# The prompt's own attention, one score step later: an edit of the order at the entry of an attention stage

## The chip, the cores and the metric

The kernel runs on one core of one Trainium2 chip. Time is device time in microseconds (us) of one execution, and the median of several runs is given. The core has five queues that work side by side, each strictly in its own order: TensorE (PE, with its weight loads shown as PEld), VectorE (DVE), ScalarE (ACT), GpSimd (POOL), and SyncE (SP), which issues the transfers. They wait for one another by semaphores.

## The reference, cut to what matters

The program is one layer of a mixer with an attention part. There are eight tiles of 128 latent tokens and one tile of 128 prompt tokens, four heads each. A latent token reads all 1,024 latent keys and 256 context keys in one softmax; a prompt token reads the 128 prompt keys only.

```python
def _block_attention(q_nope, q_ropes, key_sets):
    ...
        s = jnp.concatenate(logits, axis=-1).astype(jnp.float32) * ATTN_SCALE
        p = jax.nn.softmax(s, axis=-1).astype(v_all.dtype)
        return jnp.einsum('bhqk,bkhv->bqhv', p, v_all)
...
        attn = _block_attention(qn, (qr,), ((kn, kr, vv),))                                  # prompt
...
        attn = _block_attention(qn, (qr_rot, qr), ((kn, kr_rot, vv), (kn_c, kr_c, v_c)))     # latents
```

The values are kept in the low-rank form in which they come (128 numbers for each key); the product with the value weights `w_uv` is made afterwards, on the 128 sums of a head.

## The kernel before, in words

Before the attention lie the modulation, the projections and the group without attention (up to about 315 us of the span). Behind it lies the output projection. The attention is written as lists of steps, each with a cost; `merged` and `run` call the steps one after the other, and `later` puts the dependent instructions of other engines into the program at a time worked out from these costs. The whole part stands under a manual schedule of PE, ACT, DVE and POOL, and SP is in program order everywhere: every queue runs in the order in which the steps issued their instructions, and nothing is moved on the chip.

A latent head is a pair (tile, head). The first six are called H0 to H5 here: (0,0), (0,1), (0,2), (0,3), (1,0), (1,1). `score_steps` (L1509) gives three steps for each: two of 512 latent keys (five matmuls each, L1503 to L1507, into one of two buffers `s1`), and one of 256 context keys (the same five lines, into one half of `s2`). `softmax` (L1468) issues what follows:

- DVE takes the maximum of the 1,024 scores (L1478), then that of the 256 (L1481), and makes the shift `nb` from both (L1482).
- ACT makes two exponentials (L1488), the 256 first and then the 1,024, which frees the buffer `s1`.
- DVE adds the two sums (L1492) and takes the reciprocal (L1493).
- POOL multiplies all 1,280 probabilities by it (L1494).

A later stage takes two heads of a tile together (`value_steps`, L1534): four transposes on PE into one of two PSUM buffers (L1550), the rounded high part on ACT (L1554), the low part on DVE (L112, the helper `lo_of`), and the value products (L1574 to L1576). The prompt tile has four steps of its own in `own_steps` (L1673), kept in a list `own`:

- `own[0]`, the scores: 20 small matmuls. Then DVE takes the maxima (L1690), ACT makes four exponentials (L1694), DVE a reciprocal (L1699), POOL the multiplication (L1701).
- `own[1]`, the transposes of the probabilities (L1708, four on PE). ACT makes the high part `ph8` (L1711), DVE the low part `pl8` (L112).
- `own[2]`, the value products (L1722 to L1724, three on PE). ACT copies the result, `os8`, out of PSUM (L1728).
- `own[3]`, the product of `os8` with `w_uv` (L1737, eight on PE). DVE multiplies the result into `mixB` (L1739).

The scores of H0 and H1 and `own[0]` come first, with the last rotary transposes `q_rope_T(7)` (L1320; its last part on DVE is L1346). Then the loop runs over pairs of heads. Its first round (`c == 0`) has the scores of H2 and H3, with `own[1]` and `own[2]` put between them. Its second round has the scores of H4 and H5, `own[3]`, and the first transposes for H0 and H1:

```python
vs = value_stream(pairs[0])
merged(sc[:2] + own[3:] + vs[:1] + sc[2:3] + vs[1:2] + sc[3:5], [])
merged(vs[2:], sc[5:])
```

So PE does, from the third round's scores on: H2 (three steps), `own[1]`, H3 first and second, `own[2]`, H3 third, H4 first and second, `own[3]`, transposes 0, H4 third, transposes 1, H5 first and second, transposes 2, H5 third, value products 0, transposes 3, value products 1, transposes 4.

Of the kernel before, what the change touches and what calls it, by code (L numbers as in the profile page):

```python
# [94 lines left out]
def tile_hymba_step(ctx: ExitStack, tc: tile.TileContext, I, O):  # L95
# [12 lines left out]
    def closed(cm):  # L108
        cm.__exit__(None, None, None)

    def lo_of(lo, src, hi):
        V.tensor_tensor(lo, src, f32(hi), op=ALU.subtract)  # L112

    def pool_copy(out, in_):
        G.tensor_scalar(out, in_, 1.0, 0.0, op0=ALU.mult, op1=ALU.add)
# [96 lines left out]
    def merged(a, b):  # L212
        ta, tb = sum(x for x, _ in a) or 1.0, sum(x for x, _ in b) or 1.0
        ia = ib = 0
        da = db = 0.0
        while ia < len(a) or ib < len(b):
            if ib >= len(b) or (ia < len(a) and da / ta <= db / tb):
                da += a[ia][0]
                run(a[ia])
                ia += 1  # L220
            else:
                db += b[ib][0]
                run(b[ib])
                ib += 1
# [1095 lines left out]
    def q_rope_T(t):  # L1320
        need(("r", t))
        g, j = t // 3, t % 3
        srcs = rot[t]
        late = t >= 7
        tp = (pst if late else psa).tile([P, 512], F32, tag="t" if late else "acc", name=f"qrT{t}")
        for s_, src in enumerate(srcs):
            for pr in range(2):
                c0 = (2 * s_ + pr) * P
                T.transpose(tp[:, c0 : c0 + P], src[:, 2 * pr : 2 * pr + 2, :].rearrange("p h r -> p (h r)"), ident)
        n = len(srcs)  # L1330
        sl = slice(j * P, (j + 1) * P)
        d5 = qr[g].rearrange("p s (a b) t -> p s a b t", b=2)
        src = tp[:, : n * 256].rearrange("p (s a t) -> p s a t", s=n, a=2)

        def part(par):
            own = slice(64 * par, 64 * par + 64)
            oth = slice(64 - 64 * par, 128 - 64 * par)
            later(0.0, lambda: S.copy(d5[own, 2 - n :, :, par, sl], src[own]))
            if t == 7:
                later((2.2, 5.8)[par], lambda: low(own, oth))  # L1340
                return
            later(0.65, lambda: V.tensor_tensor(d5[oth, 2 - n :, :, par, sl], src[own], f32(d5[own, 2 - n :, :, par, sl]), op=ALU.subtract))

        def low(own, oth):
            par = own.start // 64
            V.tensor_tensor(d5[oth, 2 - n :, :, par, sl], src[own], f32(d5[own, 2 - n :, :, par, sl]), op=ALU.subtract)  # L1346

        later(0.1 if t == 7 else 0.6, lambda: part(0))
        later(0.15 if t == 7 else 1.2, lambda: part(1))
# [159 lines left out]
    def score_steps(t, h):  # L1509
        g, j = t // 3, t % 3  # L1510
        sl = slice(j * P, (j + 1) * P)
        a, b = qnh[g][:, h, sl], qnl[g][:, h, sl]
        unrot = qr[g][:, 1, h, sl]
        c_ = s2[:, h % 2, :]
        rot = qr[g][:, 0, h, sl]
        cell = {}

        def lat(half):
            if half == 0:
                cell["s"] = pss.tile([P, 2, 512], F32, tag="s1", name=f"s1{t}{h}", bufs=2)  # L1520
            logits(cell["s"][:, half, :], (a, b, rot), slice(half * 512, half * 512 + 512))
            if half == 1:
                cell["start"], cell["shift"] = softmax(t, h, cell["s"].rearrange("p a c -> p (a c)"), c_)
                later(1.2, cell["start"])

        def con():
            logits(c_, (a, b, unrot), slice(CTX0, CTX0 + 256))
            later(0.7, cell["shift"])

        return [(1.08, lambda: lat(0)), (1.08, lambda: lat(1)), (0.55, con)]  # L1530
# [77 lines left out]
    def split_job(hi, lo, key):  # L1608
        def low():
            lo()  # L1610
            made.add(key)

        def high():
            hi()
            later(1.6, lambda: los.append(low))

        his.append(high)
# [12 lines left out]
    def wo_piece(k, hi, lo):  # L1630
        woh[k], wol[k] = hi, lo
        loads.append((k, hi, lo))
        next_load()
# [26 lines left out]
    def wo_need(k):  # L1660
        while not made.issuperset((("w", k, 0), ("w", k, 1))):
            if los:
                spare_lo(1)
            elif waiting:
                now_, (due, fn) = now[0], waiting.pop(0)
                now[0] = due
                fn()
                now[0] = now_
            else:
                spare_hi(1)  # L1670
# [103 lines left out]
    with tc.manual_schedule(engines=engines):  # L1774
        mh, ml, xr, wps = {}, {}, {}, {}
        tail = []

        def mix_tiles(t):
            mh[t] = flat[0][4 + len(mh) % 2].rearrange("p (c q) -> p c q", c=8)
            ml[t] = wo.tile([P, 8, P], F32R, tag="ml", name=f"ml{t}", bufs=2)  # L1780
            sl = slice(t * P, (t + 1) * P)
            return [(mh[t][:, 4 * i : 4 * i + 4, :], ml[t][:, 4 * i : 4 * i + 4, :], src[:, :, sl]) for i, src in enumerate((mixA, mixB))]

        def mix_split(t):
            for hi, lo, src in mix_tiles(t):
                S.copy(hi, src)
                lo_of(lo, src, hi)

        def mix_jobs(t):
            for i, (hi, lo, src) in enumerate(mix_tiles(t)):  # L1790
                split_job(lambda hi=hi, src=src: pool_copy(hi, src), lambda hi=hi, lo=lo, src=src: lo_of(lo, src, hi), ("m", t, i))

        def out_terms(t, ps, c0, c1, ks):
            for k in ks:
                wo_need(k)
                a, b = mh[t][:, k, :], ml[t][:, k, :]
                T.matmul(ps, a, woh[k][:, c0:c1], start=k == 0, stop=False)  # L1797
                T.matmul(ps, a, wol[k][:, c0:c1], start=False, stop=False)  # L1798
                T.matmul(ps, b, woh[k][:, c0:c1], start=False, stop=k == NK - 1)  # L1799

        own = own_steps()
        first = [s_ for i in range(LEAD) for s_ in score_steps(*heads[i])]
        merged(first[:4] + own[:1] + [(0.45, lambda: q_rope_T(7))] + first[4:], [])
        for c in range(len(pairs)):
            sc = [s_ for i in (2 * c + LEAD, 2 * c + LEAD + 1) if i < len(heads) for s_ in score_steps(*heads[i])]
            if c == 0:
                sc = sc[:3] + own[1:2] + sc[3:5] + own[2:3] + sc[5:]
            if not sc:
                break
            if c == 1:  # L1810
# [3 lines that stand above are left out]
            else:  # L1814
                merged(sc, value_stream(pairs[c - 1]) if c > 0 else [])
            if 2 * c + LEAD + 1 == 11:
                closed(c_ra)
                c_wo, wo = opened("wo", side="left")
                for k in range(2):
                    wo_piece(k, *flat[0][2 * k : 2 * k + 2])  # L1820
                mix_jobs(8)
                mix_jobs(0)
            if 2 * c + LEAD + 1 == 23:
                for k in range(3):
                    wo_piece(2 + k, *flat[1][2 * k : 2 * k + 2])
        need(*[("e", *h) for h in heads[-2:]])
        closed(c_ps)
        c_pw, psw = opened("psw", bufs=5, space=PSUM)
        tail.append(1)
        for k, tags in ((5, ("kch", "kcl")), (6, ("krh", "krl"))):  # L1830
            wo_piece(k, *[kv.tile([P, 1024], F32R, tag=n, name=f"{n}{k}") for n in tags])
        wo_piece(7, *flat[2][0:2])
        for t in (8, 0):
            wps[t] = [psw.tile([P, 512], F32, tag="w", name=f"w{t}{i}") for i in range(2)]

        def load_xr(t):
            xr[t] = ep.tile([P, 1024], F32, tag="xr", name=f"xr{t}", bufs=4)
            nc.sync.dma_start(xr[t], I["x"][t])

        early = [  # L1840
            (0.65, lambda t=t, i=i, k=k: out_terms(t, wps[t][i], 512 * i, 512 * i + 512, [k]))
            for k in range(5) for t in (8, 0) for i in range(2)
        ]
        vs = value_stream(pairs[-2])
        merged(vs[:3], [])
        merged(vs[3:], early[:10])
        merged(value_stream(pairs[-1], drain=True), early[10:])
        catch_up(1e9)
# [181 lines left out]
```

## Time and profile before

| What | us |
|---|---|
| Median of three runs | 621.02 (620.98 to 623.31) |
| The profiled execution: span from the first to the last instruction | 620.5 |
| PE busy | 606.8 (98%) |
| PE weight loads busy | 549.0 (88%) |
| DVE busy | 411.3 (66%) |
| ACT busy | 298.9 (48%) |
| POOL busy | 123.2 (20%) |

The profile gives the span and no other time of its own for this execution; the median of the runs lies 0.5 us above the span. A line of the timeline has the start, the duration, the engine, the source line, the operation, the tile that is written and those that are read, the shape and the number of instructions merged; idle time ahead of it and what ended that stand in square brackets. Durations of matmuls overlap: the end of one is modelled, and the distance between two starts is the pace. A row of stretches gives the bounds, the length, the busy time of each engine (with the number of instructions), the granted clock of PE (1.00 is full speed), the share of the transfers and GB/s.

### The profile page before, as it was taken

What the parts mean: (1) busy time and instruction counts of PE and PEld (TensorE: products, weight loads), DVE (VectorE), ACT (ScalarE), POOL (GpSimd) and SP (SyncE); (2) the same over time, 40 slices, a digit from 0 to 9 for tenths busy, and PEclk for the clock granted to TensorE, in tenths of its full rate; (3) what the DMA queues carried; (4) which work ended last, traced back from release to release, by engine and by line L of the source; (5) the groups of instructions that cost most, each with busy time, mean ns of one, the idle gap of its engine ahead of it and who ended that gap; (6) DMA issues with size and microseconds to landing.
All of it is one profiled execution on the core that took longest, in us unless ns stands there. A gap on an engine that the chain in (4) does not pass through costs nothing.

```text
span 620.5 us, 9955 instructions
## 1 busy us (share of the span) xinstructions
PE 606.8 (98%) x3719; PEld 549.0 (88%) x3719; DVE 411.3 (66%) x938; ACT 298.9 (48%) x694; POOL 123.2 (20%) x167
## 2 busy tenths in 40 slices
PE   7999999999999999999999999999999999999995
PEld 6777889999989999999998899999999988888884
DVE  4685457997756468566778656767666754577655
ACT  6556764345433245455675565555555632232212
POOL 2461112000000000433364112323222241000001
PEclk8999999999999999999999999999999999999998
DMA  8992010100351133100010000000101113423311
GB/s 316 393 380 71 0 35 2 35 0 3 134 208 70 64 106 122 38 1 1 1 42 1 1 2 0 2 9 27 35 1 35 35 68 129 144 101 137 115 55 68
DMA packets 15327, 46.32 MB, mean 75 GB/s; under 512 B 1824, under 2 KB 4784, under 8 KB 14768
## 3 DMA queue, kind: packets, MB, share of 16 engines
q1 hardware_dynamic: 15136, 45.50, 20.7%
q8 instruction: 29, 0.48, 0.3%
q10 hardware_dynamic: 144, 0.20, 0.1%
q14 instruction: 18, 0.15, 0.1%
HBM read 40.87 MB, written 4.83 MB: 74 GB/s over the span
## 4 chain that ended last, share of the span: by engine, by line
PE 93%; DVE 3%; DMA 1%; ACT 1%; issue 1%; SPq 0%; ACTq 0%
PE p L953 10%; PE tp L751 8%; PE tp L975 5%; PE pT L1550 5%; PE w L1797 5%; PE w L1799 5%; PE w L1798 5%; PE s L1505 3%; PE s L1506 3%; PE s L1504 3%; PE s L1503 3%; PE o L1574 3%; PE s L1507 3%; PE o L1576 3%; PE o L1575 3%; PE zacc L1389 2%
## 5 line engine op out<-in xcount | busy, mean ns | idle before, releaser
L112 DVE TENSOR_TENSOR pl<-pT,ph 128x512 fp32r<-128x512 f32 x81 | 55.4, 687 | 48.8 <-ACT ph L1554 48.2
L1488 ACT ACTIVATE e<-s,nb,scl 128x256 f32<-128x256 f32 x64 | 56.1, 881 | 35.1 <-DVE nb L1482 35.1
L1494 POOL TENSOR_SCALAR e<-e,rs 128x1280 f32<-128x1280 f32 x32 | 43.0, 1343 | 130.2 <-DVE rs L1493 124.7
L1554 ACT CAST ph<-pT 128x512 fp32r<-128x512 f32 x80 | 45.5, 588 | 41.9 <-PE pT L1550 39.0
L751 PE MATMUL tp<-area,w 128*128 128x384 f32 x288 | 52.5, 338 | 0.0
L751 PEld LDWEIGHTS tp<-area,w 128*128 128x128 f32 x288 | 50.4, 188 | 0.4
L1550 PE MATMUL pT<-ident,e 128*128 128x128 f32 x320 | 48.0, 272 | 1.3 <-DVE pl L112 1.2
L1574 PE MATMUL o<-ph,vh 128*128 128x256 f32 x160 | 47.8, 299 | 0.0
L1576 PE MATMUL o<-ph,vl 128*128 128x256 f32 x160 | 44.9, 281 | 0.0
L1575 PE MATMUL o<-pl,vh 128*128 128x256 f32 x160 | 44.7, 280 | 0.0
L1799 PE MATMUL w<-area,ml 128*128 128x512 f32 (+1 forms) x114 | 43.2, 379 | 0.0
L1550 PEld LDWEIGHTS pT<-ident,e 128*128 128x128 f32 x320 | 37.4, 140 | 4.8 <-issue 1.6
L1478 DVE TENSOR_REDUCE m<-s 128x1 f32<-128x1024 f32 x32 | 38.9, 1217 | 1.5 <-PE s L1507 1.5
L1503 PE MATMUL s<-kch,area 128*128 128x512 f32 (+2 forms) x100 | 38.9, 389 | 0.0
L1236 POOL TENSOR_TENSOR kr<-z,rope 128x64 f32<-128x64 f32 x8 | 2.6, 321 | 172.0 <-ACT z L1245 172.0
L1506 PE MATMUL s<-krh,area 128*128 128x512 f32 (+2 forms) x100 | 35.4, 354 | 0.0
L1505 PE MATMUL s<-kch,area 128*128 128x512 f32 (+2 forms) x100 | 35.4, 354 | 0.0
L1504 PE MATMUL s<-kcl,area 128*128 128x512 f32 (+2 forms) x100 | 35.3, 353 | 0.0
L1507 PE MATMUL s<-krl,area 128*128 128x512 f32 (+2 forms) x100 | 35.1, 351 | 0.0
L975 PE MATMUL tp<-area,w 128*128 128x384 f32 x192 | 35.0, 337 | 0.0
L975 PEld LDWEIGHTS tp<-area,w 128*128 128x128 f32 x192 | 33.6, 188 | 0.4 <-issue 0.4
L1574 PEld LDWEIGHTS o<-ph,vh 128*128 128x128 f32 x160 | 30.1, 188 | 1.6
(375 smaller groups left out, 1601.1 us busy)
## 6 DMA issues: line engine op xcount, KB each, us to landing
ada<-in_ada_ss SPq DMA_DIRECT2D x16, 512.0 KB, 8.1
w2r<-in_w_t SPq DMA_DIRECT2D x12, 512.0 KB, 4.4
x<-in_x SPq DMA_DIRECT2D x9, 512.0 KB, 7.4
xr<-in_x SPq DMA_DIRECT2D x9, 512.0 KB, 4.0
adag<-in_ada_g SPq DMA_DIRECT2D x4, 1024.0 KB, 4.8
wor<-in_w_o SPq DMA_DIRECT2D x8, 512.0 KB, 3.4
out_y<-y SPq DMA_DIRECT2D x8, 512.0 KB, 4.8
wvr<-in_w_v SPq DMA_DIRECT2D x8, 256.0 KB, 9.2
```

The costliest lines, as they stand in the source:

```text
L112: V.tensor_tensor(lo, src, f32(hi), op=ALU.subtract)
L751: T.matmul(tps[i, g][:, :GW], w_[i][:, k, :], x_[k, g], start=k == 0 and j == 0, stop=k == NK - 1 and j == 2)
L953: T.matmul(banks[key], a_, b_, start=k == 0 and m == 0, stop=k == 3 and m == len(passes) - 1)
L975: T.matmul(tps[c, 2][:, :GW], w_[c][:, k, :], x_[k, 2], start=k == 0 and m == 0, stop=k == NK - 1 and m == 2)
L1488: S.activation(e[:, sl], src, AF.Exp, bias=nb, scale=scl[:, t : t + 1], accum_out=su[:, i : i + 1])
L1503: T.matmul(ps, qh_, kch[:, sl], start=True, stop=False)
L1505: T.matmul(ps, ql_, kch[:, sl], start=False, stop=False)
L1550: T.transpose(ps[:, w : w + P], es[t, h][:, c * P : (c + 1) * P], ident)
L1574: T.matmul(o, vh[:, kt, :], ph[:, sl], start=c == 0, stop=False)
L1575: T.matmul(o, vh[:, kt, :], pl[:, sl], start=False, stop=False)
L1576: T.matmul(o, vl[:, kt, :], ph[:, sl], start=False, stop=c == n - 1)
L1799: T.matmul(ps, b, woh[k][:, c0:c1], start=False, stop=k == NK - 1)
```

## The change

Only the order of the first round of the loop is changed. The transposes `own[1]` stand behind the first score step of H3, no longer ahead of it. The value products `own[2]` stand behind the third score step of H3, no longer ahead of it. What they issue on ACT and DVE moves with them. `own[3]` stays where it is.

```diff
             if c == 0:
-                sc = sc[:3] + own[1:2] + sc[3:5] + own[2:3] + sc[5:]
+                sc = sc[:4] + own[1:2] + sc[4:] + own[2:3]
             if not sc:
                 break
             if c == 1:
```

The instructions are the same in number and kind on every engine. Their order around the edit is this, for the queues that it changes:

| Queue | before | after |
|---|---|---|
| PE | H2 third, own[1], H3 first, H3 second, own[2], H3 third, H4 first | H2 third, H3 first, own[1], H3 second, H3 third, own[2], H4 first |
| ACT | exp H1, ph8, exp H2, os8, exp H3 | exp H1, exp H2, ph8, exp H3, os8 |
| DVE | rs H1, pl8, L1346, max H3 | rs H1, L1346, pl8, max H3 |
| DVE, later | max H4 (L1478), mixB (L1739), rs H3 | max H4 (L1478), rs H3, mixB (L1739) |

Here exp is L1488, max is L1478 and rs is L1492 with L1493. POOL and SP keep their order.

## The prediction

> **What bounds the kernel now.** I read the page first, for the bound; then stretches behind the entry; then the timeline of each engine between 324 and 343 us, row by row, because an edit of order is worth what the waits there are worth; last the granted clock.
>
> ```profile
> span 620.5 us, 9955 instructions
> PE 606.8 (98%) x3719; PEld 549.0 (88%) x3719; DVE 411.3 (66%) x938; ACT 298.9 (48%) x694; POOL 123.2 (20%) x167
> ```
>
> ```profile
> 360.00:380.00 20.00, 20.00 (x144) 18.61 (x143) 13.79 (x28) 10.76 (x22) 5.36 (x4) 1.00 0.00 1
> ```
>
> PE is the bound, and behind the entry it never stops (20.00 of 20.00 in this stretch). So what the entry gains or loses by about 346 us reaches the end of the program unchanged: nothing behind it has slack on PE to take it up, and no other engine is full there. The entry itself has two stops on PE:
>
> ```profile
> 327.10 0.66 PE L1708 MATMUL pT<-ident,e 128*128 128x128 f32 x4 [0.62 <-POOL e L1701]
> ...
> 331.21 0.40 PE L1503 MATMUL s<-kch,area 128*128 128x512 f32 x1
> ...
> 333.51 1.05 PE L1737 MATMUL at<-e,wuv 128*128 128x128 f32 x8
> ...
> 338.17 0.60 PE L1550 MATMUL pT<-ident,e 128*128 128x128 f32 x4
> ...
> 342.16 0.63 PE L1550 MATMUL pT<-ident,e 128*128 128x128 f32 x4 [0.95 <-DVE pl L112]
> ```
>
> The first stop (0.62) is the transposes of the prompt waiting for POOL. The second (0.95) ends with a low part on DVE. `own[3]` (L1737) starts at 333.51 without a wait. From it to the end of H5's second score step PE needs 338.17 - 333.51 = 4.66 us.
>
> **The change, part by part.** *The stop ahead of the transposes.* H3's first score step now comes first. It needs the buffer of H1, which the long exponential of H1 frees:
>
> ```profile
> 325.44 1.20 ACT L1488 ACTIVATE e<-s,nb,scl 128x1024 f32<-128x1024 f32 x1
> ...
> 327.80 0.59 ACT L1711 CAST ph<-pT 128x512 fp32r<-128x512 f32 x1 [1.07 <-PE pT L1708]
> ...
> 333.34 0.57 ACT L1488 ACTIVATE e<-s,nb,scl 128x256 f32<-128x256 f32 x1 [1.94 <-DVE nb L1482]
> ...
> 335.08 0.58 ACT L1554 CAST ph<-pT 128x512 fp32r<-128x512 f32 x1
> ```
>
> It ends at 325.44 + 1.20 = 326.64, so H3 starts at about 326.7 to 326.8, 0.3 to 0.4 us ahead of 327.10. The gain is 0.3 to 0.4 at most; the transposes then come at about 327.9, and their probabilities are ready (before, they were by 327.10). This gain is kept only if PE waits for nothing behind it.
>
> *ph8 and pl8.* On ACT `ph8` moves behind both exponentials of H2; on DVE `pl8` stays ahead of H3's maximum, so that maximum now waits for them.
>
> ```profile
> 327.52 0.22 DVE L1482 SCALAR_TENSOR_TENSOR nb<-m,nscl 128x1 f32<-128x1 f32 x1
> ...
> 328.47 0.69 DVE L112 TENSOR_TENSOR pl<-pT,ph 128x512 fp32r<-128x512 f32 x1 [0.46 <-ACT ph L1711]
> ...
> 330.11 1.23 DVE L1478 TENSOR_REDUCE m<-s 128x1 f32<-128x1024 f32 x1 [0.22 <-PE s L1507]
> 331.37 0.16 DVE L1492 TENSOR_TENSOR rs<-su 128x1 f32<-128x1 f32 x1
> ...
> 332.08 1.16 DVE L1482 SCALAR_TENSOR_TENSOR nb<-m,nscl 128x1 f32<-128x1 f32 x1
> ...
> 336.15 1.16 DVE L1482 SCALAR_TENSOR_TENSOR nb<-m,nscl 128x1 f32<-128x1 f32 x1
> 337.24 1.27 DVE L112 TENSOR_TENSOR pl<-pT,ph 128x512 fp32r<-128x512 f32 x2
> 338.43 1.21 DVE L1478 TENSOR_REDUCE m<-s 128x1 f32<-128x1024 f32 x1
> 339.56 0.14 DVE L1492 TENSOR_TENSOR rs<-su 128x1 f32<-128x1 f32 x1
> ```
>
> `nb` of H2 ends at 327.74, and nothing ahead of it changes. ACT is free, so H2's exponentials start at about 327.80 (0.10 behind `nb`, as at 333.34 behind 333.24, would be 327.84). The two take 335.08 - 333.34 = 1.74 until ACT begins the next: `ph8` 329.54 to 330.13. `pl8` 330.18 (328.47 stands 0.08 behind 327.80 + 0.59) plus 0.69: 330.87. H3's maximum starts about 0.1 ahead of that end, as at 338.43 ahead of 337.24 + 1.27: 330.78 in place of 330.11. The reciprocal's first part follows after 1.13 (339.56 - 338.43) to 1.26 (331.37 - 330.11): 331.95.
>
> *The value products on PE.* They need `pl8`: PE waits until about 330.92, does two of three matmuls (2 x 0.23; ten took 333.51 - 331.21), and starts H4 at 331.38 in place of 331.21. So the gain of 0.3 is gone already, and H4's scores end at 331.38 + (333.51 - 331.21) = 333.68.
>
> *os8.* This is the term that decides. On ACT `os8` now stands behind both exponentials of H3; these wait for `nb` of H3, and `nb` is held up by POOL:
>
> ```profile
> 331.89 1.34 POOL L1494 TENSOR_SCALAR e<-e,rs 128x1280 f32<-128x1280 f32 x1 [2.37 <-DVE rs L1493]
> ```
>
> `nb` took 0.22 at 327.52, but 1.16 at 332.08, and ended at 333.24, just as POOL's pass ended (331.89 + 1.34 = 333.23). POOL starts 331.89 - 331.37 = 0.52 behind the reciprocal's first part, and `nb` comes after that, now as before. So: POOL 332.47 to 333.81; `nb` ends 333.81; exponentials 333.91 (333.34 was 0.10 behind); `os8` 1.74 later, 335.65, and as long as the copy at 327.80, 0.59: 336.24. `own[3]` waits for it and starts at 336.29 in place of 333.51: 2.78 later. The small steps bound it: starts 0.03 to 0.12 behind an end and the 1.13 to 1.26 above give 336.21 to 336.48, a delay of 2.70 to 2.97. PE stands still from 333.68 to 336.29, 2.6 us.
>
> *mixB and the rest.* `mixB` moves behind H3's reciprocal on DVE and waits there for `own[3]`; behind it wait H4's second maximum, which needs PE's step after `own[3]` anyway, and the low parts of transposes 0. I cost it at nothing: POOL's pass for H3 then runs at about 336.4 to 337.7, ahead of H4's `nb`, which came 336.15 - 333.51 = 2.64 behind `own[3]` and so comes at 338.9; it then takes 0.22 and not 1.16. Without that cover `nb` stays as long as it was. L1346 moves ahead of `pl8` (nothing reads it soon). SP's and POOL's orders do not change, and no transfer is moved.
>
> *What is late next.* PE needs 4.66 to the end of H5's second step, plus 0.06 for starting after a wait (four transposes took 0.66 at 327.10, 0.60 at 338.17): 341.01. H5's maximum on DVE may start up to 0.1 sooner behind it than at 338.43, where two low parts ahead of it ended at 338.51; I take 0.06. From that maximum a chain on DVE (reciprocal, `nb` held by POOL, low part) leads to the second stop at 342.16, and every link hangs on that maximum. So the second stop stays, and does not take up the delay. Sum: 2.78 + 0.06 - 0.06 = 2.8 us, with bounds 2.7 to 3.0.
>
> **The clock.** A stop of 2.6 us raises a second question:
>
> ```profile
> 8.35:11.76 3.41, 1.60 (x19) 0.48 (x18) 1.67 (x7) 2.37 (x5) 1.33 (x1) 1.00 1.00 381
> 11.76:15.17 3.41, 3.01 (x14) 3.01 (x15) 2.59 (x4) 2.12 (x6) 1.52 (x2) 0.50 1.03 418
> 15.17:18.59 3.42, 3.42 (x13) 2.94 (x12) 3.00 (x10) 2.30 (x5) 0.00 (x0) 0.50 1.04 407
> ...
> 339.44:342.85 3.41, 2.46 (x22) 2.29 (x21) 2.51 (x6) 1.61 (x4) 1.33 (x1) 1.00 0.00 0
> ...
> 612.51:615.92 3.41, 0.56 (x5) 0.36 (x4) 2.37 (x8) 0.66 (x2) 0.96 (x1) 1.00 0.00 0
> ```
>
> PE's clock was granted at 0.50 in two stretches of this execution: from 11.76 to 18.59, and from 615.92 on. The first lasted 6.83, twice 3.41, and the two falls lie 604.16 apart, 177 times 3.413. So the clock is set at the ends of windows of 3.41 us that run through. A window with PE busy for 1.60 of 3.41 (47%) let it fall, one with 2.46 (72%) kept it, and after a fall it took one wholly busy window to come back. With a stop of 2.6 us a window is 24% busy if it holds all of it, and under 47% if it holds 1.8 of it. Where a window begins against the program I take as equally likely everywhere: at least 1.8 of the stop falls in one window in (0.8 + 2 x 0.8) of 3.41, 70%. At half speed for one window PE loses 1.7 us of work; 1.3 if the window begins up to 0.8 before the stop ends. Nearly all of it lies ahead of H5's second step (4.7 us of PE work), so it adds to the delay: 2.8 + 1.5 = 4.3 us.
>
> The Trainium skill ("TensorE: Matmul & The Clock Gate", Part 1, What's actually happening, and Why this matters for your kernels) has the clock fall after an idle window of about 3.4 us, and only gaps over about 3 us as harmful. The trace agrees on the length of the window (3.41), but its clock fell after one that was 47% busy; by the page's rule the stop here would be too short, and the time would be that of the first rival.
>
> **The rivals.**
>
> *The clock holds.* For it: only two windows of this trace tell what lets it fall, the 47% counts small matmuls at their modelled length, and the stop can lie across the end of a window, 1.3 on each side. Against it: the row of 47%. Time: 621.02 + 2.8 = 623.8, own range 623.6 to 624.1.
>
> *The clock stays low for two windows,* as at 11.76, where a window 88% busy did not bring it back. The window in which it fell here may hold the end of the stop. PE loses up to 1.7 more, less what the second stop (0.95) gives back: 626.4 to 627.
>
> *The delay is taken up (not slower).* If the second stop hung on DVE's own queue and not on H5's scores, it would give back 0.95 us and DVE's idle time. That decides only if `own[3]` is late by under about 1 us, that is if `os8` got through by 334.5. Against it: `os8` cannot start ahead of H3's exponentials, and those cannot start ahead of 333.24 even with the old times. Time: only the 0.3 of the first stop is left, 620.7.
>
> **How the numbers follow.** The sum stands against the profiled execution's span of 620.5; I add it to the median of the runs shown, 621.02, which is 0.5 above. Chances: fall for one window 0.50, clock holds 0.34, two windows 0.10, not slower 0.04, anything else 0.02. Forecast: 621.02 + 4.3 = 625.3, own range 624.9 to 625.8. The range 623.4 to 626.2 holds the first two cases and their bounds. About 0.5% (3.1 us, 624.1) is what a measurement of this kernel can tell from no change. The fall and its longer form lie above it (0.60), the upper end of the holding clock and half of the rest too (0.05): slower 0.65. The holding clock otherwise is within: 0.31. Faster: 0.04 (most of the last rival is even within).
>
> **What would show it.** Right: L1728 behind H3's exponentials and L1737 waiting for it about 2.5 us; L1711 behind H2's exponentials; L1723 waiting for L112 about 0.7; `nb` of H3 over 0.9 long; the second stop still there; all of PE 2.8 us later at transposes 4, or over 4 with a stretch at 0.50 near 336 to 341. Wrong: L1737 without a wait, the second stop gone, or a granted clock that never leaves 1.00.

## The result and the profile after

| | median us | runs |
|---|---|---|
| before | 621.83 (620.98 to 623.31) | 6 |
| after | 625.12 (623.87 to 626.44) | 6 |

The ratio after to before is 1.0057, with a 95% interval of 1.0042 to 1.0072: the changed kernel is slower by some 3.5 us.

The first lines of the page of the profiled execution after the change give the span and the busy time of each engine; the execution's own time is 625.27.

```profile
span 623.5 us, 9953 instructions
PE 607.4 (97%) x3719; PEld 549.1 (88%) x3719; DVE 410.0 (66%) x938; ACT 298.7 (48%) x694; POOL 123.0 (20%) x167
```

PE has the same 3,719 matmuls and 607.4 us of busy time (606.8 before), while the span is 3.0 longer. So PE has no more work; it stands still for longer. The view of PE's waits after the change (what it waited for, us in total, times, longest) says where:

```profile
PE at L1737 <- ACT e L1728: 2.3, 1, 2.3
...
PE pT L1550 <- DVE pl L112: 1.1, 2, 0.9
...
PE s L1503 <- ACT e L1488: 0.3, 1, 0.3
PE o L1723 <- DVE pl L112: 0.3, 1, 0.3
```

Before, the two rows of the attention were these:

```profile
PE pT L1550 <- DVE pl L112: 1.2, 2, 1.0
...
PE pT L1708 <- POOL e L1701: 0.6, 1, 0.6
```

The wait of 0.6 at the prompt's transposes is gone, a wait of 2.3 at `own[3]` (L1737) is new, and the second stop is where it was. The timelines of PE, ACT, DVE and POOL after the change answer to the rows that the prediction showed of before:

```profile
321.64 0.38 PE L1329 MATMUL qrT<-ident,qun 128*128 128x128 f32 x2
...
326.96 0.50 PE L1503 MATMUL s<-kch,area 128*128 128x512 f32 x1 [0.29 <-ACT e L1488]
...
330.41 0.41 PE L1722 MATMUL o<-ph,vh 128*128 128x512 f32 x1
331.11 0.50 PE L1723 MATMUL o<-pl,vh 128*128 128x512 f32 x1 [0.28 <-DVE pl L112]
...
331.68 0.39 PE L1503 MATMUL s<-kch,area 128*128 128x512 f32 x1
...
336.43 1.16 PE L1737 MATMUL at<-e,wuv 128*128 128x128 f32 x8 [2.31 <-ACT e L1728]
...
345.13 0.63 PE L1550 MATMUL pT<-ident,e 128*128 128x128 f32 x4 [0.91 <-DVE pl L112]
...
354.07 0.61 PE L1593 MATMUL at<-os,wuv 128*128 128x128 f32 x4
```

```profile
329.69 0.58 ACT L1711 CAST ph<-pT 128x512 fp32r<-128x512 f32 x1
334.06 0.56 ACT L1488 ACTIVATE e<-s,nb,scl 128x256 f32<-128x256 f32 x1 [3.78 <-DVE nb L1482]
...
335.79 0.58 ACT L1728 COPY e<-o 128x512 f32<-128x512 f32 x1
```

```profile
330.37 0.69 DVE L112 TENSOR_TENSOR pl<-pT,ph 128x512 fp32r<-128x512 f32 x1 [1.45 <-POOL e L1494]
330.97 1.21 DVE L1478 TENSOR_REDUCE m<-s 128x1 f32<-128x1024 f32 x1
332.10 0.15 DVE L1492 TENSOR_TENSOR rs<-su 128x1 f32<-128x1 f32 x1
...
332.81 1.15 DVE L1482 SCALAR_TENSOR_TENSOR nb<-m,nscl 128x1 f32<-128x1 f32 x1
...
339.11 0.22 DVE L1482 SCALAR_TENSOR_TENSOR nb<-m,nscl 128x1 f32<-128x1 f32 x1
```

```profile
332.62 1.34 POOL L1494 TENSOR_SCALAR e<-e,rs 128x1280 f32<-128x1280 f32 x1 [2.92 <-DVE rs L1493]
```

The reader follows the chain from the end. `own[3]` starts at 336.43, just behind `os8` (335.79 + 0.58 = 336.37). `os8` stands on ACT behind the two exponentials of H3, the first of which starts at 334.06. That waits for `nb` of H3, which took 1.15 and ended at 332.81 + 1.15 = 333.96, the moment at which POOL's pass ended (332.62 + 1.34). POOL waited for the reciprocal, that for H3's maximum on DVE, and that for `pl8`.

How much the entry lost can be read inside the traces, free of all that comes before it. The entry is measured from the last two rotary transposes (L1329, one row, 321.47 before, 321.64 after) to the first product of a latent pair with `w_uv` (L1593). That one was at 351.11 before:

```profile
321.47 0.38 PE L1329 MATMUL qrT<-ident,qun 128*128 128x128 f32 x2
...
351.11 0.61 PE L1593 MATMUL at<-os,wuv 128*128 128x128 f32 x4
```

The entry took 29.64 before and 32.43 after: 2.79 longer. The same measure is given for each experiment below, beside the ratio of its times. Up to `own[3]` it is 12.04 before (333.51 - 321.47) and 14.79 after, 2.75 longer.

### The profile page after: what moved, and what is told of

Same layout as the page of the kernel before. It is cut to its first block, busy times and chain, and to the rows that moved or that the text cites. A ratio compares the mean times of both kernels' runs of the same rounds, so it can differ in the third digit from the quotient of the medians.

```text
span 623.5 us, 9953 instructions
## 1 busy us (share of the span) xinstructions
PE 607.4 (97%) x3719; PEld 549.1 (88%) x3719; DVE 410.0 (66%) x938; ACT 298.7 (48%) x694; POOL 123.0 (20%) x167
## 4 chain that ended last, share of the span: by engine, by line
PE 92%; DVE 3%; DMA 1%; ACT 1%; issue 1%; SPq 0%; POOL 0%; ACTq 0%
PE p L953 10%; PE tp L751 8%; PE tp L975 5%; PE pT L1550 5%; PE w L1797 5%; PE w L1799 5%; PE w L1798 5%; PE o L1574 3%; PE s L1505 3%; PE s L1506 3%; PE o L1576 3%; PE s L1504 3%; PE s L1503 3%; PE s L1507 3%; PE o L1575 3%; PE zacc L1389 2%
## 5 line engine op out<-in xcount | busy, mean ns | idle before, releaser
L1488 ACT ACTIVATE e<-s,nb,scl 128x256 f32<-128x256 f32 x64 | 56.0, 880 | 37.4 <-DVE nb L1482 37.4
L1478 DVE TENSOR_REDUCE m<-s 128x1 f32<-128x1024 f32 x32 | 38.9, 1216 | 1.9 <-PE s L1507 1.9
```

Of the source, the lines that this page charges most:

```text
L1488: S.activation(e[:, sl], src, AF.Exp, bias=nb, scale=scl[:, t : t + 1], accum_out=su[:, i : i + 1])
```

## The experiments

### The changed kernel again, in more runs

No edit; the runs ask for the size of the change and for the granted clock.

> The changed kernel once more, beside the kernel before on the same chip, for the size of the change and for the clock. If only the queues count: 2.8 us over before in all runs alike (+0.45%), granted clock 1.00 around 326 to 350 us. If the clock also falls in some executions, depending on where its window of 3.41 us begins: runs in two groups, about +2.8 and +4.3, and a lower mean clock (by about 0.003) in the long ones.

Measured: 625.46 us (six runs) against 621.55 (24 runs of the kernel before), ratio 1.0063 (1.0047 to 1.0079). The entry took 32.45. The clock stayed at full speed through the stop. So the result repeats; the 2.8 us of the queues are there in both traces, and the fall of the clock in neither. Two groups some 1.5 apart cannot be made out in the six spans (623.0 to 625.0).

### The transposes alone

```diff
-                sc = sc[:4] + own[1:2] + sc[4:] + own[2:3]
+                sc = sc[:4] + own[1:2] + sc[4:5] + own[2:3] + sc[5:]
```

This stands against the changed kernel: `own[1]` is late, and `own[2]` is where it was before.

> Only the transposes own[1] stand one score step later; the value products own[2] stay between H3's second and third step. On ACT the copy os8 is then ahead of H3's exponentials, as before. If os8's place is the cause: own[3] (L1737) starts without a wait, and what is left is the wait of the value products for pl8 (behind H2's exponentials on ACT): PE at H4's first step 331.98 in place of 331.21, +0.7 us in all. If the cause is that pl8 holds up H3's maximum on DVE (and so H3's exponentials): nearly all of the 2.8 us stays.

Measured: 622.80 us (12 runs), ratio 1.0019 (1.0006 to 1.0031). The entry took 30.51, 0.87 more than before. The timelines of PE and ACT of this kernel:

```profile
329.64 0.49 PE L1722 MATMUL o<-ph,vh 128*128 128x512 f32 x1 [0.35 <-ACT ph L1711]
330.42 0.50 PE L1723 MATMUL o<-pl,vh 128*128 128x512 f32 x1 [0.29 <-DVE pl L112]
...
333.87 1.05 PE L1737 MATMUL at<-e,wuv 128*128 128x128 f32 x8
```

```profile
331.18 0.59 ACT L1728 COPY e<-o 128x512 f32<-128x512 f32 x1 [1.60 <-PE o L1724]
333.36 0.56 ACT L1488 ACTIVATE e<-s,nb,scl 128x256 f32<-128x256 f32 x1 [1.60 <-DVE nb L1482]
```

Now `os8` stands ahead of H3's exponentials, and `own[3]` doesn't wait. What is left is PE waiting for `ph8` and then for `pl8`, and the transposes' own stop has turned into a wait of 0.29 for H1's exponential.

### The value products alone

```diff
-                sc = sc[:4] + own[1:2] + sc[4:] + own[2:3]
+                sc = sc[:3] + own[1:2] + sc[3:] + own[2:3]
```

> Only the value products own[2] are moved, behind H3's third score step; the transposes stay where they were, so that ph8 and pl8 and H3's maximum are as before. os8 is behind H3's exponentials on ACT. If os8's place is the cause: own[3] waits from 333.5 to about 335.7, 2.2 us, and the kernel is 2.2 us longer. If pl8 ahead of H3's maximum is the cause: no change (within 0.3 us).

Measured: 624.89 us (7 runs), ratio 1.0056 (1.0036 to 1.0077); the entry took 31.88, 2.24 more. The timeline of PE of this kernel:

```profile
328.80 0.66 PE L1708 MATMUL pT<-ident,e 128*128 128x128 f32 x4 [0.62 <-POOL e L1701]
...
337.39 1.16 PE L1737 MATMUL at<-e,wuv 128*128 128x128 f32 x8 [2.07 <-ACT e L1728]
```

Both stops stand, the old one and the new one. So the products behind H3's third step are what puts `os8` behind H3's exponentials. The two halves don't add up: 0.87 + 2.24 = 3.11, both together 2.79. With the products late too, PE doesn't wait for `ph8`, and what it loses to `pl8` lies ahead of the longer wait for `os8`, which takes it up.

### The product with `w_uv` out of the way

```diff
-                merged(sc[:2] + own[3:] + vs[:1] + sc[2:3] + vs[1:2] + sc[3:5], [])
+                merged(sc[:2] + vs[:1] + sc[2:3] + vs[1:2] + sc[3:5] + own[3:], [])
```

This is the changed kernel with `own[3]` behind H5's second step. If the wait for `os8` is the cost, giving PE other work meanwhile must take it away.

> The changed kernel with own[3] moved too: behind H5's two large score steps, so that PE has other work while os8 waits on ACT. If PE's stop at own[3] is what costs: L1737 starts without a wait, and the kernel comes back to about +0.4 us over before; what is left is DVE's chain to transposes 4, with H4's shift (L1482) now under POOL's pass again. If the delay sits in the chain of H3's exponentials itself and not in PE's stop: it stays at +2 us or more.

Measured: 621.99 us (12 runs), ratio 1.0004 (0.9993 to 1.0015), no change from before; the entry took 30.07, 0.43 more. The timeline of PE of this kernel:

```profile
336.93 1.05 PE L1737 MATMUL at<-e,wuv 128*128 128x128 f32 x8
...
339.68 0.39 PE L1574 MATMUL o<-ph,vh 128*128 128x256 f32 x1 [0.67 <-DVE mixB L1739]
```

`own[3]` starts without a wait. The products behind it now wait 0.67 for `mixB`, which is late instead. That is more than the 0.43 that is left; on the other side the second stop, 0.95 before, is gone in this kernel.

### The POOL pass of H2 one step later

```diff
-            later(2.5 if t == 0 or (t, h) < (1, 2) else 1.9, divide)
+            later(4.2 if (t, h) == (0, 2) else 2.5 if t == 0 or (t, h) < (1, 2) else 1.9, divide)
```

The changed kernel again, but the reciprocal and division of H2 come into the program later, so that `nb` of H3 stands ahead of them. The link by which POOL held `nb` is cut, and the reciprocal's two small instructions no longer stand ahead of `nb` either.

> The changed kernel with the reciprocal of H2 (L1492, L1493) behind H3's shift (L1482) on DVE, so that POOL's pass over H2's probabilities starts after the shift. If POOL's pass holds up the shift: L1482 of H3 takes 0.22 us in place of 1.15, H3's exponentials, os8 and own[3] come about 1.3 us sooner, and the kernel is about 1.5 us over before in place of 2.8. If the shift is long for a reason of its own: it stays at 1.15, and only the 0.3 us of the two small instructions ahead of it are won.

Measured: 624.09 us (12 runs), ratio 1.0034 (1.0022 to 1.0046); the entry took 31.21, 1.57 more instead of 2.79. The timelines of DVE and PE of this kernel:

```profile
332.88 0.22 DVE L1482 SCALAR_TENSOR_TENSOR nb<-m,nscl 128x1 f32<-128x1 f32 x1
```

```profile
335.57 1.16 PE L1737 MATMUL at<-e,wuv 128*128 128x128 f32 x8 [1.08 <-ACT e L1728]
```

`nb` takes 0.22 in place of 1.15, and the wait at `own[3]` falls from 2.31 to 1.08. Counted from L1329, `nb` ends 1.20 sooner than in the changed kernel: 0.93 of it is POOL's hold (1.15 less 0.22), and 0.27 is its earlier start (10.90 in place of 11.17 behind L1329), with the reciprocal out of its way. So the hold on DVE is 0.9 of the 2.8.

### The order of before, with both of its stops removed

The same idea, applied to the kernel before:

```diff
-                later((2.2, 5.8)[par], lambda: low(own, oth))
+                later((5.2, 5.8)[par], lambda: low(own, oth))
...
-            later(2.5 if t == 0 or (t, h) < (1, 2) else 1.9, divide)
+            later(4.2 if (0, 2) <= (t, h) < (1, 1) else 2.5 if t == 0 or (t, h) < (1, 2) else 1.9, divide)
```

The first line moves a low part of the last rotary transposes on DVE (the one ahead of the prompt's softmax), the second the divisions of H2 to H4.

> The kernel before, with two edits of the order on DVE: the first of the two L1346 behind the reciprocal of the prompt's sums (L1699) and H2's shift, and the reciprocals of H2, H3 and H4 (L1492, L1493) behind the shift (L1482) of the head after them. If the two stops of PE in the kernel before come from this order, the stop at the transposes (0.62) shrinks to about 0.2, the shifts take 0.22 in place of 1.16, the stop at transposes 4 (0.95) goes, and the kernel is about 1.5 us faster than before (-0.25%). If the stops have other causes: no change.

Measured: 620.30 us (12 runs) against 621.56 (23 runs), ratio 0.9973 (0.9961 to 0.9985): faster than both kernels. The entry took 27.87, 1.77 less than before. In the view of PE's waits of this kernel, only this row of the attention is left, a wait at 504.15, far behind the entry:

```profile
PE pT L1550 <- DVE pl L112: 0.2, 1, 0.2
```

So the stop of 0.62 can be had back without moving the transposes, and the second stop of 0.95 came from the order on DVE as well. The shifts `nb` of H3 and H4 take 0.22 here, so the hold by POOL is gone with it; the two edits were not tried one by one, and what each is worth is not shown.

### Twelve stops of known length

The kernel before with stops put into PE's queue ahead of later pairs: a transpose, 8 to 18 copies of its result on ACT, and a transpose of the copy, for which PE waits. The results aren't used.

```diff
+        def stop(c, n):
+            ps = pst.tile([P, 512], F32, tag="t", name=f"stop{c}")
+            T.transpose(ps[:, 0:P], ident, ident)
+            d = ap_.tile([P, 512], F32R, tag="ph", name=f"dz{c}", bufs=4)
+            for _ in range(n):
+                S.copy(d[:, 0:P], ps[:, 0:P])
+            T.transpose(ps[:, P : 2 * P], f32(d[:, 0:P]), ident)
...
+            if c >= 3:
+                run((0.0, lambda: stop(c, (8, 11, 14, 18)[c % 4])))
```

> The kernel before with twelve stops on PE, one ahead of each round of the attention from the fourth to the fifteenth: PE transposes a block, ACT copies it 8, 11, 14 or 18 times, PE transposes the copy. PE stands still for about 1.5 to 4 us each time, at places that fall differently against the clock's window of 3.41 us. It computes the same and does more. If a window with PE busy for under about half lets the clock fall: stretches at 0.50 behind every stop that leaves a window under about 47% busy, some eight of the twelve, each costing up to 1.7 us beside the stop. If only a window that is idle, or nearly, does: none, or only behind stops over 3 us.

Measured (one run): 693.2 us. The stops were 2.50, 3.39, 4.28 and 5.47 us, three of each, longer than expected, and the clock fell after all twelve. So no window between 35% and 50% busy was tried in the attention. Rows of stretches of this kernel: the second begins where the granted clock falls and ends where it comes back, the first and third are the windows of 3.41 beside it, and the first holds the larger part of a stop of 2.50:

```profile
375.53:378.95 3.42, 1.21 (x6) 1.04 (x7) 0.29 (x2) 3.20 (x11) 0.00 (x0) 1.00 0.00 0
378.95:382.36 3.41, 3.41 (x17) 3.22 (x16) 0.92 (x3) 1.07 (x3) 0.33 (x1) 0.50 0.02 5
382.36:385.78 3.42, 3.42 (x26) 3.23 (x26) 2.24 (x3) 1.55 (x3) 1.01 (x1) 1.00 0.00 0
10.31:13.72 3.41, 2.18 (x24) 1.24 (x25) 1.52 (x4) 2.02 (x4) 2.36 (x2) 1.00 1.04 420
```

A window 35% busy (1.21 of 3.42) let the clock fall, for one window. So a stop of 2.5 us, about the length of ours (2.31), can do it. The last row is of the program's start, the window ahead of a fall at 13.72: there a window with PE 64% busy by the profile, with small matmuls of 128x32, fell as well.

### The stop filled with matmuls

```diff
+        def filler():
+            ps = pst.tile([P, 512], F32, tag="t", name="filler")
+            for i in range(10):
+                T.matmul(ps, vh[:, NS, :], kch[:, 0:512], start=i == 0, stop=i == 9)
...
-                merged(sc[:2] + own[3:] + vs[:1] + sc[2:3] + vs[1:2] + sc[3:5], [])
+                merged(sc[:2] + [(0.0, filler)] + own[3:] + vs[:1] + sc[2:3] + vs[1:2] + sc[3:5], [])
```

The changed kernel with ten matmuls, whose result isn't used, in the place of the stop: the same delay, but PE busy.

> The changed kernel with ten further matmuls (128x512, about 2.3 us, result unused) on PE between H4's second score step and own[3], where PE otherwise stands still for 2.3 to 2.7 us. The queues and own[3]'s start stay as in the changed kernel; only PE is busy in the stop. If the clock falls behind the stop in some executions and that is what lifts the measured change from 2.8 to 3.5 to 3.9 us: the kernel is 2.8 us over before (+0.45%), no longer, and some of its runs have a mean clock of 0.995 or more, as before's do. If the clock has no part in it: 3.5 to 3.9 us over before, as the changed kernel.

Measured: 625.15 us (9 runs), ratio 1.0039 (1.0024 to 1.0054). The entry took 32.42, as in the changed kernel. The timeline of PE of this kernel:

```profile
334.17 2.43 PE L1804 MATMUL filler<-kch,vh 128*128 128x512 f32 x10
336.65 1.16 PE L1737 MATMUL at<-e,wuv 128*128 128x128 f32 x8
```

In the mean of the spans this kernel lies 2.7 above the kernel before (622.76 against 620.06), the changed one 3.4 (623.45). The 0.7 between them has the sign that a falling clock would give, but it is no more than such a comparison of 9 and 14 runs can tell. The mean clocks point the same way, as the first of the two expectations has it: three of these nine executions have 0.997 and one 0.993, while of the 14 of the changed kernel one has 0.996 and eight 0.993 to 0.994.

### The clock in further executions, and the stop moved against the windows

These two are the changed kernel without an edit, for the clock at the stop.

> The changed kernel, one more execution with a profile, to see a stop that lies otherwise against the clock's window. The rule so far (windows with PE busy for 35% or less fell, 50% or more held): a stretch at 0.50 behind the stop at own[3] if a window has under about 45% there, none otherwise. From the entry to transposes 4, 2.8 us more than before without the stretch, about 4.3 with it.

> As the look before it: the changed kernel, one more execution with a profile. A stretch at 0.50 behind own[3]'s stop if a window has PE busy for under about 45%, and then about 4.3 us more than before from the entry to transposes 4; none and 2.8 us otherwise.

Measured: 625.52 and 624.08 us. In neither did the clock fall at the stop. The row of the window ahead of a possible fall, in the first and in the second:

```profile
332.65:336.07 3.42, 1.74 (x8) 1.10 (x6) 2.75 (x4) 1.76 (x5) 1.34 (x1) 1.00 0.00 0
```

```profile
331.15:334.56 3.41, 1.78 (x8) 1.13 (x6) 2.80 (x4) 1.71 (x4) 1.34 (x1) 1.00 0.00 0
```

With 51% and 52% busy the clock held. The end of a window cut the stop in two in both, as in the first profile of the changed kernel, where the two windows around it were 50% and 82% busy:

```profile
332.41:335.83 3.42, 1.70 (x8) 1.08 (x6) 2.74 (x4) 1.77 (x5) 1.34 (x1) 1.00 0.00 0
335.83:339.24 3.41, 2.81 (x23) 2.78 (x24) 1.56 (x5) 1.28 (x4) 1.33 (x1) 1.00 0.02 5
```

Nine matmuls were then put ahead of the attention's first scores, in the changed kernel and in the one before, to move the stop by 2 us against the windows:

```diff
+        def ahead():
+            ps = pst.tile([P, 512], F32, tag="t", name="ahead")
+            for i in range(9):
+                T.matmul(ps, kch[:, 0:P], kch[:, 0:512], start=i == 0, stop=i == 8)
+
+        run((0.0, ahead))
```

> The changed kernel with nine further matmuls (128x512, about 2.1 us, result unused) on PE ahead of the first scores of the attention. They move the stop at own[3] by 2.1 us against the clock's window, whose ends lay near 332.4, 335.8 and 339.2 in the profiles that showed no fall. The stop then lies at about 336.1 to 338.5, all in one window, which is some 30% busy. If the clock's window decides: a stretch at 0.50 of 3.4 us behind the stop in the profile if its window begins as in those, and from own[3] to transposes 4 about 1.6 us more than in the changed kernel (there 8.70). If stops of 2.3 us never let the clock fall: granted clock 1.00, and 8.70.

> The kernel before with the same nine matmuls at the same place, as the measure for the shifted changed kernel: about 2.1 us over before or less, where another engine hides a part. The shifted changed kernel should lie 2.8 us above it without a fall of the clock, and up to 4.5 where the clock falls.

Measured: 629.59 us (5 runs) in the changed order, ratio to the kernel before 1.0122 (1.0104 to 1.014), and 624.37 (6 runs) in the order of before, ratio 1.0051 (1.0032 to 1.007). The entry took 32.45 and 29.64, as without the nine. But the nine also waited 1.14 for a part of the keys, so the shift was about 3.5 us (L1329 comes 10.16 behind L1368 in place of 6.67), a whole window, and the stop was cut in two again (2.28 and 2.23 of 3.41 busy). The profile shows no fall. So this pair doesn't tell what a stop in one window does. Its two kernels lie 4.3 apart in the mean of 5 and 6 runs (5.2 by the medians), where their entries differ by 2.81; at the same mean clock, 0.990 to 0.991, the spans lie 3.0 apart (627.97 in three runs, 624.95 in two).

## Why the prediction was right, and where it was not

The side was right, and the time of 625.3 was met within 0.2; but of its two terms only the queues are shown, and that the time came so close is in part luck.

- *The first stop.* The gain of 0.3 to 0.4 came, and was spent at once. H3 started at 326.96; less 0.17, by which this execution reached the entry later, that is 326.79 (the forecast stands in brackets, here and below: 326.7 to 326.8). It waited there 0.29 for H1's exponential.
- *ph8 and pl8.* In the same reckoning `ph8` started at 329.52 (329.54), `pl8` at 330.20 (330.18), H3's maximum at 330.80 (330.78).
- *The products.* The low-part product started at 330.94 (330.92), H4 at 331.51 (331.38). The wait shows as 0.28, not 0.7: the matmul ahead of it is drawn 0.41 long, and only the 0.70 between the two starts, against a pace of 0.23, tells the loss of about 0.5.
- *os8, the term that decides.* POOL started at 332.45 (332.47), the exponentials at 333.89 (333.91), `os8` at 335.62 (335.65), `own[3]` at 336.26 (336.29). It is late by 2.75 where 2.78 was said. The wait of PE there is drawn 2.31 long and not 2.6: H4's scores began 0.13 later than said, and the last matmul ahead is drawn 0.39 long where the pace is 0.23. The value products alone, the late `own[3]` and the late division each change the entry as this chain says, so the chain is shown and not only argued.
- *What is late next.* The second stop stayed (0.91), `nb` of H4 fell to 0.22, `mixB` cost nothing (H4's second maximum behind it still waited 0.34 for PE), and the entry ended 2.79 late: the sum of 2.8 was right. The rival in which the delay is taken up fell.
- *The clock: the step that the traces don't bear out.* The prediction added 1.5 for one window at half speed, as the likeliest course. None of the four traces of the changed kernel, nor that of its shifted form, shows a fall; the term measured 0 there. The row it was built on, 47% busy at the program's start, counts small matmuls, and a window there 64% busy fell as well, while at the entry 50% to 52% was enough to hold. So the bound of 1.8 us of stop in one window, and the chance of 70% worked out from it, had no fair row. An estimate from the rows of the runs: with a stop of 2.31, a fall where 2.21 of it lies in one window (the row that fell) and none where 1.72 does (the row that held), the same sum gives 38 to 67%. It still takes every place of the window as equally likely, and in all five of these traces a window's end cut the stop in two. In these traces the rival in which the clock holds is what happened.
- *The base: an error the other way.* The prediction added its sum to the median of three runs, 621.02. The mean of 71 further runs of the kernel before is 621.84, 0.8 more. And the times lie about 1.8 above the span in every run (625.27 against 623.5), so that the profiled execution of before was one of some 622.3 us, not 621.02. 621.84 + 2.79 is 624.6; the 14 runs of the changed kernel have a mean of 625.24. So the base was 0.8 too low, and the 1.5 for the clock was 0.9 more than the 0.6 that the runs leave over. The two errors nearly cancel: that is the luck in the hit.

The 0.6 that is left stays open. It may be the clock after all, in part of the executions. One window at half speed lowers the mean clock of an execution by 0.5 x 3.41/623 = 0.0027. The 71 executions of before have 0.990 to 0.991 (30) or 0.995 to 0.998 (35), and 6 lie between. Of the 14 of the changed kernel, ten lie one such step lower, and the four whose traces were kept, each the first of its series, don't:

| mean clock, after | executions | mean span | above before at | by |
|---|---|---|---|---|
| 0.996 | 1 | 622.30 | 0.995 to 0.998 (619.46) | 2.8 |
| 0.990 to 0.991 | 3 | 623.87 | 0.990 to 0.991 (620.93) | 2.9 |
| 0.993 to 0.994 | 8 | 623.09 | 0.995 to 0.998 (619.46) | 3.6 |
| 0.987 to 0.988 | 2 | 624.85 | 0.990 to 0.991 (620.93) | 3.9 |

By this a fall would come in ten of 14 and cost 0.8 to 1.0, not 1.5. Against it: the value products alone have three executions at 0.993 to 0.994 that lie only 2.1 above before, which is their queues' 2.24 and no fall (its two at 0.988, on the other hand, lie 4.1 above). Nor need one such step be a fall at the stop: the six executions of before that lie between stand at 0.993, with a mean span of 619.18, no longer than the rest, and the kernel with twelve stops has a low stretch of one window at its start, from 13.72. A trace of one of the ten would decide, and there is none. So a falling clock is pointed to and not shown.

## What to carry to other kernels

When a step is moved in a program with strict queues, follow each instruction it issues to the queue it lands on and ask what stands ahead of it there: here a copy of 0.58 us on an engine that is 48% busy cost 2.2 us by itself, and 2.8 with the transposes moved too, since it came to stand behind two exponentials whose shift another engine held up. Look for the hold before moving the step: issuing the pass on POOL and a low part on DVE somewhat later made the kernel before 1.3 us faster by the medians and its entry 1.77 shorter, with the order on PE untouched. And take the base of a forecast from more than three runs, or from the same trace as the sum.

## What the runs showed of the hardware

*A tiny operation waits inside its own duration.* `nb`, 128x1 from two operands in SBUF, takes 0.22 us, and 1.15 when POOL's pass over 128x1280 runs; it ends with that pass. The profile draws this as busy time of DVE and not as a wait, so no view of waits shows it. The Trainium skill ("SBUF — State Buffer", Who interferes with whom) says that a DVE instruction with two inputs in SBUF contends with a GpSimd instruction that reads SBUF, through a shared port that is held exclusively; the traces agree (1.15 beside the pass, 0.22 ahead of it in the kernel with the later pass).

*A stop shorter than a window can let the clock fall.* It fell after all twelve stops of 2.50 to 5.47 us, six of them shorter than a window (2.50 and 3.39), each time at the end of a window at most 35% busy; behind windows 50% to 52% busy it held. The low stretch was 3.41 long behind stops up to 4.28, and 6.83 behind the three of 5.47. The busy share alone doesn't say when it comes back: behind the last stop a low window 82% busy (2.81 of 3.41) was enough, at the start of the kernel before one 88% busy (3.01) was not. The Trainium skill ("TensorE: Matmul & The Clock Gate", Why this matters for your kernels) warns only of gaps over about 3 us; here the clock fell behind stops of 2.50, which are shorter, and the measurement decides.

*The same kernel has two times, and the mean clock tells them apart.* Executions of the kernel before with a mean clock of 0.990 to 0.991 have spans of 620.93, those with 0.995 to 0.998 of 619.46, 1.5 apart. The traces of the first kind have a stretch at half speed near 12 to 18 us, and those of the second kind (the transposes alone, for one) have none. What decides whether the stretch comes, and that it alone costs the 1.5, no run here shows.
